# A hybrid decoder layer on one core: the norm of k as a part of its own ahead of the head pair's stage

## The chip, the core and the metric

The kernel runs on one core of a Trainium2 chip. The metric is the device time of one execution in microseconds (us); three runs of the kernel before took 1516.64, 1517.29 and 1518.45 us, the median is 1517.29 us. Five engines work side by side, each through its own queue in order: TensorE (PE for matmuls, PEld for its weight loads), VectorE (DVE), ScalarE (ACT), GpSimd (POOL) and SyncE (SP, which here only issues DMAs).

## What is computed

One layer of a decoder for a prompt of 512 tokens and 8 single-token samples, 520 columns in all, with 1024 channels. Two feed-forward blocks stand around a mixing block; the change lies in the mixing block alone, in the branch with a recurrent state. Cut to what matters here:

```python
h = rmsnorm(x, norm_mix);  z = h @ w_in              # 8448 columns: r | k | v | lora | conv B, C, u | gates
r, k, v, wd, ad, gd = token_shift(z_rwkv)
w = -softplus(-(decay_bias + tanh(wd) @ w_decay_up)) - 0.5;  decay = exp(-exp(w))
a = sigmoid(iclr_bias + ad @ w_iclr_up)
kk = heads(k * k_k)                                  # 16 heads of 64 channels
kk = kk / max(norm(kk, axis=-1), 1e-12)              # the norm that the change moves
k_mod = k * (1 + (a - 1) * k_a)
for t in range(T):                                   # per head, S is 64 x 64
    S = S * decay[t] - (S @ kk[t]) x (kk[t] * a[t]) + v[t] x k_mod[t]
    y[t] = S @ r[t]
```

The norm is a sum of 64 squares for each token and head, and the reciprocal root of it, by which `k * k_k` is then scaled.

## The kernel before

Activations lie with channels on the partitions, so a tile is 128 channels by 520 columns and holds two heads. A product with a block of 128 output columns of `w_in` is two halves of 260 columns, each 8 channel tiles by 3 matmuls (high by high, high by low, low by high part), 24 matmuls into one PSUM bank (lines 795 to 797). In the text one of these matmuls is called a step. Each half is read out of its bank by ACT and DVE before one of the three banks of the tag `mm` is used again.

`mix` (line 730) holds the mixing block, in which parts are Python generators, and a planner at its end (lines 1323 to 1386) writes them into one program. The parts are: `rkv(p)` makes k, then r, then v of head pair p (three products; `zshift` puts the shifted copy into the one buffer `mp` by ACT, line 808, and blends it by DVE, line 812); `conv` and `gate` are the other products; `stage(p)` prepares the recurrence of pair p in chunks of 32 tokens; `invert(p)` inverts the chunk's triangular matrices (32 x 32, many small DVE steps on the tile `F`, lines 1082 to 1093); `scan(q)` runs the 16 chunks for two pairs; `fin(p)` normalises its output; `sample` treats the 8 samples. Each `yield a, b` tells the planner how much TensorE time the lines above take by its reckoning, and how long to wait until this part goes on; a part starts when those named in `needs` are done. The products of one row ("big") fill the gaps, so that the planner lays the small matmuls of a stage between the steps of products. After that every engine takes its instructions in the order in which they stand in its queue.

`stage(p)` has four places that the text speaks of. **D**: the two small products for decay and rate (line 945, two halves, each with two banks of the tag `mw`), whose banks two tanh passes on ACT free (lines 946, 947). **K**: five small matmuls (line 968) that sum the squares, made by an ACT pass at the stage's start (line 943), per head and token; DVE then does the norm's Newton steps, 12 instructions of 104 x 10 elements (line 972 and the helper `rsqrt`, lines 49 to 54). **R**: ten small matmuls (line 995) that spread the norm back over 128 rows, into both banks of `mw`, and DVE multiplies k by it (line 998). **S**: 32 small matmuls for the chunk's inner products (line 1013), which need the chain of DVE passes after D: lines 951, 953, 988, 998, 1000, 1002, 1004 and 1005. So D, K, R and S stand in TensorE's queue in this order, with steps of products between them.

Of the kernel before, what the change touches and what calls it, by code (L numbers as in the profile page):

```python
# [8 lines left out]
F32 = mybir.dt.float32  # L9
F32R = mybir.dt.float32r  # L10
I32 = mybir.dt.int32
AF = mybir.ActivationFunctionType
ALU = mybir.AluOpType
AX = mybir.AxisListType

P = 128
D = 1024
NT = 8
# [27 lines left out]
def rsqrt(eng, pool, x, y):  # L46

    a = pool.tile([P, 16], F32, tag="nwt", name="nwt", bufs=2)[:x.shape[0], :x.shape[1]]
    eng.tensor_scalar(y.bitcast(I32), x.bitcast(I32), 1, None, ALU.logical_shift_right)
    eng.tensor_scalar(y.bitcast(I32), y.bitcast(I32), -1, 0x5F3759DF, ALU.mult, ALU.add)  # L50
    for _ in range(3):
        eng.scalar_tensor_tensor(a, y, -0.5, y, ALU.mult, ALU.mult)
        eng.tensor_tensor(a, a, x, ALU.mult)
        eng.scalar_tensor_tensor(y, a, 1.5, y, ALU.add, ALU.mult)


def hybrid_step(tc, I, O):
# [3 lines left out]
    with ExitStack() as top:  # L61
# [551 lines left out]
        with tc.tile_pool(name="mx", bufs=1) as mp:  # L613
# [12 lines left out]
            def wo_part():  # L626
# [13 lines left out]

            out = []
            mix(tc, nc, mp, pp, dp, low0, wprep, mwps, mmps, V, VV, I, O, HS, YM, ysplit, wo_part,
                ident, pmask)

# [85 lines left out]
def mix(tc, nc, mp, pp, dp, low0, wprep, mwps, mmps, V, VV, I, O, HS, YM, ysplit, wo_part, ident, pmask):  # L730

    hh, hl = [a for a, _ in HS], [b for _, b in HS]
    v1, act, pool = nc.vector, nc.scalar, nc.gpsimd
# [35 lines left out]
    def tt(name, bufs=1, w=N):  # L769
        return mp.tile([P, w], F32, tag=name, name=name, bufs=bufs)  # L770
# [4 lines left out]
    def c3(ap):  # L775
        return ap.rearrange("p (c t) -> p c t", t=C)
# [38 lines left out]
    zz, done = {}, {}  # L815
# [90 lines left out]
    GT = 104  # L906
    GROUPS = (slice(0, 4 * GT), slice(4 * GT, N))

    def parts(src, hi, lo):

        act.activation(hi, src, AF.Identity)
        pool.tensor_tensor(lo, src, hi.bitcast(F32), ALU.subtract)
        return hi, lo

    def t2(name, w=N, tags=(None, None)):
        return [mp.tile([P, w], F32R, tag=t or name + x, name=name + x) for x, t in zip("hl", tags)]

    def small(w, x, cs, name, rows=slice(0, P)):

        ps = mwps(name)  # L920
        terms = [(w[0], x[0]), (w[0], x[1])] + [(y, x[0]) for y in w[1:]]
        for i, (a, b) in enumerate(terms):
            nc.tensor.matmul(ps[:, :HN], lhsT=a[rows], rhs=b[rows, cs], start=i == 0, stop=i == len(terms) - 1)
        return ps[:, :HN]
# [5 lines left out]
    heads = blkr.bitcast(F32).rearrange("p (h x) -> p h x", h=2)[:, :, 0]  # L930
    ups = {}

    def wdi_load(p):
        raw = tt("wdi", 1, P)
        nc.sync.dma_start(raw, I["wdi"][:, p * P:(p + 1) * P])
        ups[p] = parts(raw, *t2("wd", P))

    def stage(p):

        r, k, vv = zz.pop(p)  # L940
        wdi = ups.pop(p)
        sg, a, kn = tt("sg"), tt("a"), tt("kn")
        act.activation(kn, k, AF.Square, scale=V("k_k", p))
        for cs in HALF:
            ps, ps2 = (small(wdi, lora, cs, x, rows) for x, rows in zip(("dec", "icl"), HP))
            act.activation(sg[:, cs], ps, AF.Tanh, bias=hka[:, 2, p:p + 1], scale=0.5)
# [15 lines left out]
        km = tt("km")  # L962
        act.activation(km, a, AF.Identity, scale=hka[:, 0, p:p + 1], bias=hka[:, 1, p:p + 1])
        pool.tensor_tensor(km, km, k, ALU.mult)

        ps = mwps("kn")
        for i in range(5):
            nc.tensor.matmul(ps[:GT, 2 * i:2 * i + 2], lhsT=kn[:, i * GT:i * GT + GT], rhs=heads, start=True, stop=True)
        rs = mp.tile([P, 10], F32, tag="rs", name="rs", bufs=2)
        yield 0.5, 0.5  # L970
        rx = mp.tile([P, 10], F32, tag="rx", name="rx", bufs=2)
        v1.tensor_scalar(rx[:GT], ps[:GT, 0:10], 1e-24, None, ALU.max)
        rsqrt(v1, mp, rx[:GT], rs[:GT])
        yield 0.0, 2.0
        if p > 3:
            yield ("fin", p - 4) if p % 2 else ("gate", p - 3)
        yield ("r", p)
# [8 lines left out]
        lam = mp.tile([P, NC], F32, tag="lam", name="lam", bufs=4)  # L986
        v1.tensor_copy(lam, eL[:, :, C])
        v1.tensor_tensor(AR[:, :, 1, :], c3(r[:, :T]), eL[:, :, 1:], ALU.mult)
        kk = kn
        kps = [mwps("kn") for _ in GROUPS]  # L990
        for cs, ps in zip(GROUPS, kps):
            for g in range(cs.start, cs.stop, GT):
                i = g // GT
                for h, hp in enumerate(HP):
                    nc.tensor.matmul(ps[hp, g - cs.start:g - cs.start + GT], rhs=ident[:GT, :GT], start=True, stop=True,
                                     lhsT=rs[:GT, 2 * i + h:2 * i + h + 1].broadcast_to([GT, 64]))
# [318 lines left out]
    def ys(m):  # L1315
# [7 lines left out]
    LAG = 1.2  # L1323
    WIN, DENSE, LIGHT = 8.0, 5500, 0.3
    make = {"scan": scan, "invert": invert, "stage": stage, "fin": fin, "sample": lambda p: sample(),
            "rkv": rkv, "conv": conv, "gate": gate, "low": lowrank, "ys": ys, "wo": lambda p: wo_part()}
    each = lambda kind: [(kind, p) for p in range(NT)]
    todo = {"scan": [("scan", q) for q in range(NT // 2)], "invert": each("invert"), "stage": each("stage"), "fin": each("fin"),
            "sample": [("sample", 0)], "ys": each("ys"), "big": []}
    bigs = {"gate": each("gate"), "rkv": each("rkv"), "conv": each("conv"), "wo": [("wo", 0)]}  # L1330
    live = {}

    def needs(kind, p):
        return {"stage": [("k", p)],
                "invert": [("stage", p)],
                "scan": [("invert", 2 * p), ("invert", 2 * p + 1)],
                "fin": [("scan", p // 2)] + [("gate", p - 2)] * (p > 1),
                "sample": [("stage", NT - 1)],
                "ys": [("gate", p), ("sample", 0)] + [(x, NT - 1) for x in ("rkv", "conv", "gate")],
                "wo": [("gate", NT - 1), ("conv", NT - 1)],  # L1340
                "rkv": [("stage", p - 2)] * (p > 1),
                "gate": [("fin", p)]}.get(kind, [])

    def ok(key):
        return all(x in done for x in needs(*key))
# [5 lines left out]
    while any(todo.values()) or any(bigs.values()) or live:  # L1351
# [5 lines left out]
        for row, q in todo.items():  # L1357
            if row not in live and q and ok(q[0]):
                key = q.pop(0)
                live[row] = [max([t] + [done[x] for x in needs(*key)]), make[key[0]](key[1]), key, None]  # L1360
# [120 lines left out]
```

## Time and profile before

The profiled execution took 1518.29 us, with a span of 1516.5 us from its first instruction to its last.

| engine | busy, us | share of the span |
|---|---|---|
| PE (matmul) | 1446.9 | 95% |
| PEld (weight load) | 1390.4 | 92% |
| DVE | 1076.5 | 71% |
| ACT | 770.1 | 51% |
| POOL | 398.5 | 26% |
| SP | issues DMAs only | |

The chain that ended last runs through PE for 75% of the span and through DVE for 15%. The mixing block takes up the stretch from about 405 to 1030 us. A row of the timeline is: start and duration in us, engine, line, operation, the tile written and the tiles read, and, in brackets, how long the engine had been idle before and what ended that. Matmuls overlap in the records, so their starts tell the pace, not their durations.

### The profile page before, as it was taken

The numbers are of one execution on the slowest core, as the hardware profiler recorded it, in microseconds if no ns is written. First come the engines' busy times: TensorE is split into PE (matmuls) and PEld (weight loads), VectorE is DVE, ScalarE is ACT, GpSimd is POOL, SyncE is SP. The second block draws the span as 40 slices with busy tenths as digits, with TensorE's granted clock in tenths as the row PEclk, the third lists the DMA queues.
The fourth block names the chain that finished last, engine by engine and source line by source line (L and its number), as shares of the span: only waits on it lengthen the run. The fifth ranks groups of instructions, "written<-read, shape, count | busy, mean of one in ns | idle before, by whom it ended". The sixth has DMA issues, their size and how long they took to land.

```text
span 1516.5 us, 36191 instructions
## 1 busy us (share of the span) xinstructions
PE 1446.9 (95%) x14772; PEld 1390.4 (92%) x14772; DVE 1076.5 (71%) x2349; ACT 770.1 (51%) x1352; POOL 398.5 (26%) x447
## 2 busy tenths in 40 slices
PE   8799999999999999999899999998989999999996
PEld 7799999999988988989888897898979999999996
DVE  7976665665698877859887659855697665666566
ACT  7655555555633443634444352244475555555643
POOL 1324334334231211201320113311023334333401
PEclk9899999999998999999999999999999999999998
DMA  5678888888332322313222222325246887888823
GB/s 180 153 167 182 181 183 183 182 191 181 123 106 68 82 66 53 97 45 83 67 67 66 73 78 87 100 88 168 91 125 161 178 185 176 192 180 172 169 68 103
DMA packets 116709, 193.44 MB, mean 128 GB/s; under 512 B 41992, under 2 KB 51208, under 8 KB 116288
## 3 DMA queue, kind: packets, MB, share of 16 engines
q1 hardware_dynamic: 92928, 140.80, 30.4%
q0 software_dynamic: 23616, 50.34, 20.7%
q8 instruction: 116, 1.90, 0.5%
q14 instruction: 49, 0.40, 0.1%
HBM read 179.83 MB, written 11.01 MB: 126 GB/s over the span
## 4 chain that ended last, share of the span: by engine, by line
PE 75%; DVE 15%; ACT 3%; issue 3%; DMA 2%; POOL 1%; SPq 0%; DVEq 0%; ACTq 0%; POOLq 0%
PE big L171 16%; PE big L173 16%; PE big L172 16%; PE big L795 6%; PE big L796 6%; PE big L797 5%; DVE lo L132 2%; PE xy L1171 1%; PE ds L1186 1%; PE xy L1177 1%; ACT hi L130 1%; PE ft L1123 1%; PE xy L1154 1%; DVE F L1090 1%; ACT W L1127 1%
## 5 line engine op out<-in xcount | busy, mean ns | idle before, releaser
L130 ACT ACTIVATE hi<-raw 128x512 fp32r<-128x512 f32 (+2 forms) x427 | 318.5, 749 | 323.6 <-PE big L172 171.2
L795 PE MATMUL big<-xh,hi 128*128 128x260 f32 x1040 | 310.5, 299 | 1.7 <-ACT cc L847 1.0
L797 PE MATMUL big<-xh,lo 128*128 128x260 f32 x1040 | 299.6, 289 | 2.0 <-DVE lo L132 2.0
L796 PE MATMUL big<-xl,hi 128*128 128x260 f32 x1040 | 300.8, 289 | 0.0
L132 DVE TENSOR_TENSOR lo<-raw,hi 128x512 fp32r<-128x512 f32 (+2 forms) x263 | 239.2, 912 | 62.1 <-ACT hi L130 57.0
L795 PEld LDWEIGHTS big<-xh,hi 128*128 128x128 f32 x1040 | 199.8, 192 | 11.6 <-ACT cc L847 1.2
L171 PE MATMUL big<-hh,hi 128*128 128x260 f32 x704 | 203.6, 289 | 3.0 <-DVE x L470 3.0
L797 PEld LDWEIGHTS big<-xh,lo 128*128 128x128 f32 x1040 | 199.3, 192 | 4.2 <-DVE lo L132 2.3
L796 PEld LDWEIGHTS big<-xl,hi 128*128 128x128 f32 x1040 | 200.1, 192 | 2.8
L172 PE MATMUL big<-hl,hi 128*128 128x260 f32 x704 | 199.5, 283 | 0.0
L173 PE MATMUL big<-hh,lo 128*128 128x260 f32 x704 | 199.5, 283 | 0.0
L171 PE MATMUL big<-th,hi 128*128 128x260 f32 x640 | 183.1, 286 | 8.5 <-ACT th L319 5.2
L172 PE MATMUL big<-tl,hi 128*128 128x260 f32 x640 | 182.8, 286 | 3.6 <-DVE tl L320 3.4
L173 PE MATMUL big<-th,lo 128*128 128x260 f32 x640 | 181.8, 284 | 0.0
L470 DVE SCALAR_TENSOR_TENSOR x<-big,x 128x260 f32<-128x260 f32 x176 | 74.5, 426 | 94.9 <-PE big L173 94.9
L171 PEld LDWEIGHTS big<-hh,hi 128*128 128x128 f32 x704 | 133.3, 189 | 6.5 <-DVE x L470 3.5
L173 PEld LDWEIGHTS big<-hh,lo 128*128 128x128 f32 x704 | 133.3, 189 | 0.0
L172 PEld LDWEIGHTS big<-hl,hi 128*128 128x128 f32 x704 | 133.2, 189 | 0.0
L171 PEld LDWEIGHTS big<-th,hi 128*128 128x128 f32 x640 | 121.5, 190 | 10.1 <-ACT th L319 6.0
L172 PEld LDWEIGHTS big<-tl,hi 128*128 128x128 f32 x640 | 121.6, 190 | 4.8 <-DVE tl L320 4.8
L171 PE MATMUL big<-xh,hi 128*128 128x260 f32 x400 | 114.9, 291 | 8.4 <-ACT hi L130 5.5
L166 DVE TENSOR_TENSOR raw<-raw 128x512 f32<-128x512 f32 x160 | 113.9, 713 | 12.6 <-DMA raw<-in_wu 5.6
(306 smaller groups left out, 3439.4 us busy)
## 6 DMA issues: line engine op xcount, KB each, us to landing
raw<-in_win SPq DMA_DIRECT2D x66, 512.0 KB, 3.8
raw<-in_wd SPq DMA_DIRECT2D x80, 256.0 KB, 2.9
lo<-in_wd POOLq DMA_DIRECT2D x72, 256.0 KB, 4.6
raw<-in_wu SPq DMA_DIRECT2D x24, 512.0 KB, 3.7
raw<-in_wg SPq DMA_DIRECT2D x23, 512.0 KB, 3.8
raw<-in_wg SPq DMA_DIRECT2D x40, 256.0 KB, 3.5
raw<-in_wu SPq DMA_DIRECT2D x40, 256.0 KB, 3.0
lo<-in_wg POOLq DMA_DIRECT2D x18, 512.0 KB, 5.7
```

The source lines that it names most:

```text
L130: nc.scalar.activation(self.hi[:, ks], self.raw[:, ks], AF.Identity)
L132: self.eng.tensor_tensor(self.lo[:, ks], self.raw[:, ks], self.hi[:, ks].bitcast(F32), ALU.subtract)
L166: nc.vector.tensor_tensor(self.raw, a.raw, b.raw, ALU.add)
L171: nc.tensor.matmul(ps[:, :HN], lhsT=hi, rhs=x[0], start=first, stop=False, skip_group_check=True)
L172: nc.tensor.matmul(ps[:, :HN], lhsT=hi, rhs=x[1], start=False, stop=False, skip_group_check=True)
L173: nc.tensor.matmul(ps[:, :HN], lhsT=lo, rhs=x[0], start=False, stop=last, skip_group_check=True)
L470: nc.vector.scalar_tensor_tensor(X[m][:, cs], ps, 0.5, X[m][:, cs], ALU.mult, ALU.add)
L795: nc.tensor.matmul(ps[:, :HN], lhsT=hi[:, k, :], rhs=hh[k][:, cs], start=k == 0, stop=False)
L796: nc.tensor.matmul(ps[:, :HN], lhsT=hi[:, k, :], rhs=hl[k][:, cs], start=False, stop=False)
L797: nc.tensor.matmul(ps[:, :HN], lhsT=lo[:, k, :], rhs=hh[k][:, cs], start=False, stop=k == nk - 1)
L1090: v1.tensor_tensor(f, f, ft[:, :, q0:, :j], ALU.add)
L1123: nc.tensor.matmul(ps[qd, i * 128:i * 128 + 96], lhsT=GM[qd, i, 96:], rhs=GM[qd, i, 0:96], start=False, stop=True, skip_group_check=True)
```

## The change

The square, K and the Newton steps leave `stage` and become a generator `norm(p)`, a row of its own in the planner. It needs only k of pair p, and `stage(p)` now needs `norm(p)`. The squares go into a tile of the tag `gt` (one buffer, also used by the lowrank, conv and gate products) in place of `kn`; the reciprocal roots wait in `rss`. Within the stage the yield that was 2.0 long in the planner's reckoning, with the one for K ahead of it, becomes one of 0.5, and `kn` is first written at line 998's multiplication.

```diff
+    rss = {}
+
+    def norm(p):
+
+        k = zz[p][1]
+        sq = tt("gt")
+        act.activation(sq, k, AF.Square, scale=V("k_k", p))
+        yield 0.0, 0.8
+        ps = mwps("kn")
+        for i in range(5):
+            nc.tensor.matmul(ps[:GT, 2 * i:2 * i + 2], lhsT=sq[:, i * GT:i * GT + GT], rhs=heads, start=True, stop=True)
+        rs = mp.tile([P, 10], F32, tag="rs", name="rs", bufs=2)
+        yield 0.5, 0.5
+        rx = mp.tile([P, 10], F32, tag="rx", name="rx", bufs=2)
+        v1.tensor_scalar(rx[:GT], ps[:GT, 0:10], 1e-24, None, ALU.max)
+        rsqrt(v1, mp, rx[:GT], rs[:GT])
+        rss[p] = rs
+        yield 0.0, 2.0
+
     def stage(p):
 
         r, k, vv = zz.pop(p)
         wdi = ups.pop(p)
-        sg, a, kn = tt("sg"), tt("a"), tt("kn")
-        act.activation(kn, k, AF.Square, scale=V("k_k", p))
+        sg, a = tt("sg"), tt("a")
...
         pool.tensor_tensor(km, km, k, ALU.mult)
-
-        ps = mwps("kn")
-        for i in range(5):
-            nc.tensor.matmul(ps[:GT, 2 * i:2 * i + 2], lhsT=kn[:, i * GT:i * GT + GT], rhs=heads, start=True, stop=True)
-        rs = mp.tile([P, 10], F32, tag="rs", name="rs", bufs=2)
-        yield 0.5, 0.5
-        rx = mp.tile([P, 10], F32, tag="rx", name="rx", bufs=2)
-        v1.tensor_scalar(rx[:GT], ps[:GT, 0:10], 1e-24, None, ALU.max)
-        rsqrt(v1, mp, rx[:GT], rs[:GT])
-        yield 0.0, 2.0
+        yield 0.0, 0.5
         if p > 3:
             yield ("fin", p - 4) if p % 2 else ("gate", p - 3)
         yield ("r", p)
...
-        kk = kn
+        kk, rs = tt("kn"), rss.pop(p)
...
     def needs(kind, p):
-        return {"stage": [("k", p)],
+        return {"norm": [("k", p)],
+                "stage": [("norm", p)],
                 "invert": [("stage", p)],
```

What this does to the queues is seen best at two places. In TensorE's queue of stage 5 before, D (`icl`) is followed by K (`kn<-blkr`, after the transposes `yt` of a `fin` part), and R (`kn<-cst,rs`) comes only after 31 steps more:

```order
L923 MATMUL icl<-lora_5319,wdh 128x260
L923 MATMUL icl<-lora_5318,wdl 128x260
L795 MATMUL big<-xh_4982,hi 128x260
L796 MATMUL big<-xl_4983,hi 128x260
L1228 MATMUL yt<-cst,AR 64x64 x16
L968 MATMUL kn<-blkr,kn 104x2 x5
L797 MATMUL big<-xh_4982,lo 128x260
```

In the same queue at the same stage after the change, where line 1004 is what was 995:

```order
L923 MATMUL icl<-lora_5319,wdh 128x260
L923 MATMUL icl<-lora_5318,wdl 128x260
L796 MATMUL big<-xl_4975,hi 128x260
L797 MATMUL big<-xh_4974,lo 128x260
L795 MATMUL big<-xh_4976,hi 128x260
L796 MATMUL big<-xl_4977,hi 128x260
L797 MATMUL big<-xh_4976,lo 128x260
L1004 MATMUL kn<-cst,rs 64x104 x10
```

R now follows D after five steps; K has left this place and stands 29 steps behind the last step of k's product, in the second half of r's. In VectorE's queue of stage 6 before, the last Newton steps (`nwt`, `rs`) stand among `invert` steps on `F`, a weight's low part (`lo`) and the reading out of a gate (`ym`), all ahead of line 988's multiplication:

```order
L54 SCALAR_TENSOR_TENSOR rs<-nwt,rs 104x10
L1088 TENSOR_TENSOR ft<-F_5326,Mr 128x2x3x5
L52 SCALAR_TENSOR_TENSOR nwt<-rs 104x10
L132 TENSOR_TENSOR lo<-raw,hi 128x1024
L53 TENSOR_TENSOR nwt<-nwt,rx 104x10
L895 SCALAR_TENSOR_TENSOR ym_5279<-gt,AR 128x252
L54 SCALAR_TENSOR_TENSOR rs<-nwt,rs 104x10
L900 SCALAR_TENSOR_TENSOR gS<-gt,gS 128x8
L988 TENSOR_TENSOR AR<-r,eL 128x16x32
```

In VectorE's queue of pair 6 after the change, the steps stand right behind the blending of k (first row), and line 952, once 972, is their first:

```order
L812 SCALAR_TENSOR_TENSOR k<-big,omm,mp 128x260
L952 TENSOR_SCALAR rx<-kn 104x10
L812 SCALAR_TENSOR_TENSOR r<-big,omm,mp 128x260
L49 TENSOR_SCALAR rs<-rx 104x10
L50 TENSOR_SCALAR rs<-rs 104x10
L52 SCALAR_TENSOR_TENSOR nwt<-rs 104x10
```

The first half of r now stands behind the step that waits for K.

## Rows read from the trace of the kernel before

**Rows 1.** Windows: busy us (count) of PE, PEld, DVE, ACT, POOL; clock; DMA.

```profile
405.00:1030.00 625.00, 598.30 (x7938) 552.92 (x7937) 482.49 (x1255) 264.36 (x538) 128.10 (x194) 0.98 0.28 79
```

**Rows 2.** The same view, five windows of 10 us.

```profile
450.00:460.00 10.00, 6.51 (x48) 5.61 (x46) 8.96 (x39) 4.17 (x10) 0.96 (x4) 0.88 0.35 113
460.00:470.00 10.00, 10.00 (x56) 10.00 (x56) 6.81 (x23) 4.79 (x11) 2.39 (x5) 0.60 0.28 51
...
770.00:780.00 10.00, 7.32 (x55) 6.88 (x54) 9.34 (x36) 3.32 (x7) 0.71 (x1) 0.76 0.18 52
780.00:790.00 10.00, 10.00 (x123) 9.79 (x123) 7.62 (x20) 2.13 (x5) 3.95 (x5) 0.90 0.28 66
1020.00:1030.00 10.00, 10.00 (x85) 10.00 (x85) 4.07 (x6) 3.75 (x7) 0.00 (x0) 1.00 0.23 68
```

**Rows 3.** Waits of PE, 405 to 1030: total us, times, longest us.

```profile
PE kn L995 <- DVE rs L54: 5.2, 2, 2.7
PE dec L923 <- ACT sg L946: 3.4, 2, 2.8
...
PE kn L995 <- DVE mp L811: 1.9, 1, 1.9
```

**Rows 4.** Groups by line: shapes, count | busy us, mean ns | idle before, releaser.

```profile
L1013 PE MATMUL sc<-AR,BK 64*64 64x64 f32 x512 | 17.1, 219 | 1.2 <-DVE BK L1005 1.2
...
L953 DVE TENSOR_TENSOR_SCAN sg<-smask,sg 128x512 f32<-128x512 f32 x8 | 11.0, 1380 | 0.0
L995 PE MATMUL kn<-cst,rs 104*64 104x104 f32 x160 | 9.8, 273 | 7.0 <-DVE rs L54 5.2 <-DVE mp L811 1.9
L968 PE MATMUL kn<-blkr,kn 128*104 128x2 f32 x80 | 9.1, 239 | 0.1
...
L946 ACT ACTIVATE sg<-dec,hka 128x260 f32<-128x260 f32 x16 | 7.6, 474 | 5.5 <-PE icl L923 3.8 <-PE dec L923 1.4
...
L943 ACT ACTIVATE kn<-k,vec 128x520 f32<-128x520 f32 x8 | 5.8, 726 | 6.9 <-PE bon L923 4.1 <-DVE k L812 2.9
L1002 DVE SCALAR_TENSOR_TENSOR a<-a,kn 128x520 f32<-128x520 f32 x8 | 5.5, 691 | 0.0
...
L52 DVE SCALAR_TENSOR_TENSOR nwt<-rs 104x10 f32<-104x10 f32 x24 | 4.0, 165 | 0.2
```

**Rows 5.** Timeline of stage 6, from its second D to its R.

```profile
766.03 0.28 PE L923 MATMUL icl<-lora,wdl 64*128 64x260 f32 x1
...
769.37 0.42 DVE L951 TENSOR_SCALAR sg<-sg 128x520 f32<-128x520 f32 x1
...
769.71 0.21 DVE L1088 TENSOR_TENSOR ft<-F,Mr 128x36 f32<-128x36 f32 x1
...
775.21 0.16 DVE L54 SCALAR_TENSOR_TENSOR rs<-nwt,rs 104x10 f32<-104x10 f32 x1
...
775.52 0.79 PE L995 MATMUL kn<-cst,rs 104*64 104x104 f32 x6 [2.69 <-DVE rs L54]
```

**Rows 6.** Timelines of pairs 1 and 6: last steps of k, its blending, its square.

```profile
444.15 0.28 PE L797 MATMUL big<-xh,lo 128*128 128x260 f32 x1
...
450.34 0.49 DVE L812 SCALAR_TENSOR_TENSOR k<-big,omm,mp 128x260 f32<-128x260 f32 x1
...
450.86 0.73 ACT L943 ACTIVATE kn<-k,vec 128x520 f32<-128x520 f32 x1 [2.87 <-DVE k L812]
...
450.88 0.39 PE L795 MATMUL big<-xh,hi 128*128 128x260 f32 x1 [0.69 <-DVE k L812]
...
457.77 0.48 ACT L808 ACTIVATE mp<-big,vec 128x260 f32<-128x260 f32 x1 [4.23 <-DVE F L1090]
...
458.67 0.58 PE L923 MATMUL dec<-lora,wdh 64*128 64x260 f32 x1 [2.79 <-ACT sg L946]
...
732.43 0.28 PE L797 MATMUL big<-xh,lo 128*128 128x260 f32 x1
...
736.80 0.48 DVE L812 SCALAR_TENSOR_TENSOR k<-big,omm,mp 128x260 f32<-128x260 f32 x1
```

More of the change, by code (lines that the diff above doesn't have):

```diff
@@ L1325, in mix @@
     make = {"scan": scan, "invert": invert, "stage": stage, "fin": fin, "sample": lambda p: sample(),
-            "rkv": rkv, "conv": conv, "gate": gate, "low": lowrank, "ys": ys, "wo": lambda p: wo_part()}
+            "rkv": rkv, "conv": conv, "gate": gate, "low": lowrank, "norm": norm, "ys": ys, "wo": lambda p: wo_part()}
     each = lambda kind: [(kind, p) for p in range(NT)]
-    todo = {"scan": [("scan", q) for q in range(NT // 2)], "invert": each("invert"), "stage": each("stage"), "fin": each("fin"),
+    todo = {"scan": [("scan", q) for q in range(NT // 2)], "invert": each("invert"), "norm": each("norm"), "stage": each("stage"), "fin": each("fin"),
             "sample": [("sample", 0)], "ys": each("ys"), "big": []}
```

## The prediction, made before the changed kernel was run

> **What bounds the kernel now.** I read the windows first, then TensorE's waits, then the groups by line and two pieces of the timeline. From 405 to 1030 us, the mixing block, PE is busy for 598.3 of 625 us and DVE for 482.5 [rows 1]: TensorE bounds this stretch, and an edit is worth only what it takes from PE's idle time or gives back to its clock. In a window without a wait PE starts 85 steps in 10 us [rows 2], 0.12 us a step.
>
> Of PE's waits in the block the largest one belongs to this change: R stands idle for the last Newton step, 5.2 us in two places and 1.9 in a third, where DVE had another small copy in hand [rows 3]. S, a little later in a stage, waits 1.2 us for the last pass of its DVE chain [rows 4]. Together that is 8.3 us. Stage 6 shows how it comes about: its second D ends at 766.31, DVE takes up the stage at 769.37 and the norm's last step ends at 775.37; R starts at 775.52 after 2.69 us of idle PE [rows 5]. The windows from 770 to 790 then show clocks of 0.76 and 0.90 [rows 2], a mixture of its two levels, 1.2 and 2.4 GHz; that cost 2.4 + 1.0 = 3.4 us more. So the most that can go is 11.7 us.
>
> The rest of PE's waits have another cause: DVE is late as such. In pair 1, k's last step starts at 444.15 but k is blended only at 450.83, 6.7 us later; PE then waits 0.69 us for the bank, and at D 2.79 us, since the tanh passes stand on ACT behind a shift copy that had waited 4.23 us for DVE [rows 6]. The clock of 0.88 and 0.60 there [rows 2] costs 1.2 + 4.0 = 5.2 us.
>
> **The change part by part.** No work is added. The square is the same ACT pass (0.73 us), K the same matmuls (9.1 / 8 = 1.1 us a stage), the Newton steps the same 12 short instructions (line 52's take 165 ns) [rows 4]. The norm issues no DMA, nothing of it runs on POOL, and nothing moves past SP's queue. Costed at nothing: the square's new tile `gt`, because in every stage the last reader of it in the program comes before k; if ACT had to wait for it, the price would be about one such pass, 0.73 us. What counts is where things now stand.
>
> *R.* In the order of the changed kernel, the norm is done long before R, which stands 12 steps behind D in stages 0, 1, 2 and 6, fewer in 3 and 5. R needs two banks of `mw`, and D's two tanh passes of 0.47 us each [rows 4] free them, so 12 steps (1.4 us) are enough and five (0.6 us) are about 0.5 us short. All of the old 7.1 us at R can go.
>
> *S.* But S moves closer to D as well, from 69 to 99 steps down to 44 to 92 (stage 4 aside, which waits for a gate), and DVE's chain between them is only relieved of the short Newton steps. For each stage I summed DVE's queue from line 951 to the chain's last pass: each instruction by the mean of its line, from the scan's 1380 ns over the passes of about 690 (five like line 1002's) down to 165, less 0.08, because a next one starts that much before the recorded end (769.71 against 769.79) [rows 4, 5]. To it comes the way from D through the second tanh, 1.2 us at best. Against it stand TensorE's steps at 0.12, R at 9.8 / 8 = 1.2 and whatever else lies between. Stage 6 after the change: 25 instructions, 8.8 us, plus 1.2 is 10.0, against 66 steps and R, 9.1: S waits 0.8. The others: 0.5 (stage 0), none (1), 1.5 (2), 0.8 (3), none (4), 0.6 (5), 0.7 (7). That is 4.9 us. The same sum on the old order gives 4.1 at R and S, where 8.3 were measured, so it is a low end. With the delay from D to line 951 that each stage showed before (3.06 us in stage 6 [rows 5], 0.5 to 4.0 in the others) the new order gives 8.7. I take the middle, 6.8: DVE's shortage in a stage mostly stays, and PE meets it at S instead of at R.
>
> *K.* This wait is new. Before, PE reached K without a wait (0.1 us in all [rows 4]), since k was done long ago. Now K stands 19 to 35 steps behind k's last step (81 in pair 3), and there k must first pass the shift copy on ACT, the blending on DVE and the square on ACT. From k's last step to the blended k took 2.3 to 7.5 us in the eight pairs, 6.7 in pair 1 and 4.9 in pair 6 [rows 6]; square and handovers add 0.9. Pair 1: 7.6 against 31 steps, 3.7 us: PE waits 3.9. Pair 6: 5.8 against 30 steps, 3.6: it waits 2.2. In the same way 0.7 in pairs 2 and 5 each; none in the others, where more steps, S or pieces of a scan lie between. That is 7.5 us. Behind K in PE's queue stand the products of r, and behind line 952 in DVE's queue the blending of r, whose bank PE needs two halves later; the square holds up the next shift copies on ACT, as it did before (2.87 us in pair 1 [rows 6]). The low end is nothing: part of this is the same lateness of DVE that PE already meets later, and in pair 1 the 0.69 and 2.79 us would be paid at K instead. Taking off these two I get 4.0, which I use.
>
> By the Trainium skill, "TensorE: Matmul & The Clock Gate", part 2, step by step, matmuls stay in program order and only weight loads are pulled ahead. The trace agrees: at 450.88 a product that waits for its bank holds up all behind it [rows 6]. If matmuls could pass K, K would cost nothing and the sum below would come out 4.0 lower; by the rule it is what it is.
>
> *Clock.* The two waits of 2.7 and 2.8 us were followed by stretches at the lower level [rows 2, 5, 6]. With waits at K of up to 3.9 us I give back half of the 3.4 us, 1.7; the ends are nothing and another stretch like that of pair 1, 5.2.
>
> *Sum*, against the profiled execution of 1518.29 us (its span of 1516.5 and 1.8 around it), which lies 1.0 above the median; differences carry over, so I add them to the median of 1517.3: -8.3 (R and S) - 3.4 (clock) + 6.8 (S) + 4.0 (K) + 1.7 (clock) = +0.8. **1518.1 us.** What lies behind is that the planner packs the stages into less product work: the last `fin` now comes 66 steps earlier, and these steps are left for the end of the block, where PE was busy for 10.00 us in a window with DVE at 4.07 [rows 2]. There they fill nothing, while DVE has the same work over a shorter run of steps.
>
> **The rivals.** *Faster:* R's waits go and DVE, freed of the chain through K, makes up for it: S waits only 4.9, K not at all, the clock stays up. -8.3 - 3.4 + 4.9 = -6.8, **1510.5**. For it: R's three waits are real, and in stage 6 the norm's last step ended 6.0 us after DVE had taken up line 951 (769.37 to 775.37 [rows 5]), which is long for 12 short instructions. Against it: k's lateness in pairs 1 and 6 [rows 6].
>
> *Slower:* K takes the place of R. PE stands in its queue for a k that has not yet come through ACT and DVE. Its whole price is 7.5 and S costs 6.8; the clock falls as often as before: -8.3 + 6.8 + 7.5 = +6.0, **1523.3**. It decides from about 4.5 us at K on. With S at 8.7 it is +7.9, 1525.2.
>
> *It does not do what it says:* K and the Newton steps could have stayed next to R if the scheduler had put them back. The order excludes it; 0.02, with no change in time.
>
> **How the numbers follow.** About 0.2%, 3.0 us, is what a measurement of this kernel can tell from no change. Unchanged (1514.3 to 1520.3) 0.36, and the 0.02 goes with it; faster 0.30; slower 0.32. The terms known to within 4 us each leave 1 in 10 below 1509.5 and 1 in 10 above 1527, the slower case with the high end of S (+7.9) and the 1.7 of the clock on top; the range reaches to these.
>
> **What would show it.** Right, if in the changed kernel line 1004 (R) has no more than 1.5 us of idle PE before it, line 1022 (S) 5 to 9 us, and line 948 (K) 2 to 8 us, most of it in pairs 1 and 6, released by ACT's square. The faster case is shown by S and K below 6 us together; the slower one by K above 4.5 us, and half clock behind it. What would make it wrong altogether: waits of the scans and of `sample`, which I leave as they are although the order changes there too, since nothing in the rows gives a direction.

## The result, and the profile of the changed kernel

The changed kernel takes 1536.4 us (median of six runs, 1530.8 to 1548.5) against 1517.2 for the kernel before; the ratio is 1.0132, with a 95% interval of 1.0103 to 1.0160. It is slower, by 19 us, and outside the range that I gave (1509.5 to 1527).

The profiled execution took 1542.6 us, 6 above the median; its span is 24.0 longer than that of before. First the PE lines of the two pages (busy us, share of the span, instructions), before and after; the spans are 1516.5 and 1540.5.

```profile
PE 1446.9 (95%) x14772; PEld 1390.4 (92%) x14772; DVE 1076.5 (71%) x2349; ACT 770.1 (51%) x1352; POOL 398.5 (26%) x447
```

```profile
PE 1457.0 (95%) x14772; PEld 1399.0 (91%) x14772; DVE 1081.8 (70%) x2349; ACT 762.4 (49%) x1346; POOL 393.6 (26%) x448
```

The same 14772 matmuls keep PE busy for 10.1 us more, and the rest of the span, in which PE stands, grew from 69.6 to 83.5, by 13.9. So there are two losses of like size: PE stands longer, and it takes longer over the same work. All of it lies in the mixing block. The windows that answer to [rows 1] and [rows 2], the second at the places where the changed kernel waits:

```profile
405.00:1030.00 625.00, 585.74 (x7746) 538.59 (x7745) 477.93 (x1240) 249.51 (x520) 124.25 (x192) 0.96 0.27 75
```

```profile
440.00:450.00 10.00, 7.37 (x64) 7.16 (x62) 9.59 (x22) 4.31 (x9) 1.84 (x5) 1.00 0.44 107
450.00:460.00 10.00, 10.00 (x74) 9.59 (x73) 8.33 (x46) 2.82 (x6) 0.72 (x3) 0.83 0.28 93
740.00:750.00 10.00, 7.19 (x42) 7.19 (x43) 8.73 (x19) 3.27 (x8) 2.65 (x4) 0.66 0.23 66
...
800.00:810.00 10.00, 8.13 (x44) 8.13 (x45) 6.80 (x25) 1.21 (x2) 0.29 (x2) 0.66 0.27 59
```

PE's mean clock in these 625 us went from 0.98 [rows 1] to 0.96. The block itself ends some 24 us later than before. Now PE's waits, 405 to 1052 us (total us, times, longest), which answer to [rows 3]; then the groups by line that answer to [rows 4]:

```profile
PE kn L948 <- ACT gt L944: 7.4, 4, 2.6
PE gu L923 <- DVE kn L1007: 5.3, 1, 5.3
PE ds L1195 <- DVE UV L1189: 5.2, 9, 1.2
PE big L797 <- DVE lo L132: 4.1, 6, 1.1
PE ft L1132 <- issue: 3.0, 4, 1.3
```

```profile
L1022 PE MATMUL sc<-AR,BK 64*64 64x64 f32 x512 | 16.6, 219 | 1.6 <-DVE ft L1097 1.6
...
L948 PE MATMUL kn<-blkr,gt 128*104 128x2 f32 x80 | 9.0, 238 | 7.4 <-ACT gt L944 7.4
L1004 PE MATMUL kn<-cst,rs 104*64 104x104 f32 x160 | 8.9, 258 | 0.0
...
L944 ACT ACTIVATE gt<-k,vec 128x520 f32<-128x520 f32 x8 | 5.8, 725 | 20.4 <-DVE k L812 20.4
```

R (line 1004) waits nowhere any more; 7.0 of idle time stood there before [rows 4]. D's 3.4 us behind ACT [rows 3] are gone too. K (line 948) waits 7.4; S (line 1022) waits 1.6, by the profile for a step of `invert` (`ft`) on DVE and not for its own chain; ACT stands 20.4 us at the Squares (line 944) for k, where 2.9 of 6.9 were for k before [rows 4]. The rest is at places the change doesn't name: `gu` of `fin` waited 1.1 and 0.2 before and waits 5.3, the scan's `ds` 1.5 and now 5.2, `big` behind `lo` 2.0 and now 4.1. These rows of before were not shown ahead:

```profile
PE big L797 <- DVE lo L132: 2.0, 2, 1.1
...
PE ds L1186 <- DVE UV L1180: 1.5, 3, 1.0
...
PE gu L923 <- ACT AR L1230: 1.1, 1, 1.1
```

How K comes to wait is seen in pair 1, at the place that answers to [rows 6] (start, duration, engine, line; in brackets the idle time ahead and what ended it):

```profile
446.61 1.23 DVE L132 TENSOR_TENSOR lo<-raw,hi 128x1024 fp32r<-128x1024 f32 x1
...
448.02 0.49 DVE L812 SCALAR_TENSOR_TENSOR k<-big,omm,mp 128x260 f32<-128x260 f32 x1
...
448.61 0.73 ACT L944 ACTIVATE gt<-k,vec 128x520 f32<-128x520 f32 x1 [3.27 <-DVE k L812]
...
449.39 1.08 PE L948 MATMUL kn<-blkr,gt 128*104 128x2 f32 x10 [2.63 <-ACT gt L944]
```

DVE has transposes and `lo` in its queue ahead of the blending of k; ACT stands 3.27 us at the Square for it, PE 2.63 at K for the Square. In stage 5, which answers to [rows 5] for R, R runs without a wait right behind D, and then holds both banks of `mw` until DVE, busy with `invert`, then with a `lo`, a gate and the stage's own first passes, comes to the kk multiply:

```profile
735.38 1.11 PE L1004 MATMUL kn<-cst,rs 104*64 104x104 f32 x20
...
742.13 0.85 DVE L1007 SCALAR_TENSOR_TENSOR kn<-k,vec,kn 128x416 f32<-128x416 f32 x2
...
742.81 0.58 PE L923 MATMUL gu<-sgd,guh 128*128 128x260 f32 x1 [5.29 <-DVE kn L1007]
```

### The profile page after: what moved, and what is told of

It reads as the page before. It is cut to its first block, busy times and chain, and to the rows that moved or that the text cites. A ratio compares the mean times of both kernels' runs of the same rounds, so it can differ in the third digit from the quotient of the medians.

```text
span 1540.5 us, 36162 instructions
## 1 busy us (share of the span) xinstructions
PE 1457.0 (95%) x14772; PEld 1399.0 (91%) x14772; DVE 1081.8 (70%) x2349; ACT 762.4 (49%) x1346; POOL 393.6 (26%) x448
## 5 line engine op out<-in xcount | busy, mean ns | idle before, releaser
L171 PEld LDWEIGHTS big<-th,hi 128*128 128x128 f32 x640 | 121.4, 190 | 10.1 <-ACT th L319 6.0
```

The costliest lines, as they stand in the source:

```text
L171: nc.tensor.matmul(ps[:, :HN], lhsT=hi, rhs=x[0], start=first, stop=False, skip_group_check=True)
```

## The experiments

All runs, with the median, the ratio to the kernel before (95% interval), and from the profiled execution PE's busy time and the rest of its span. The last column is counted from the timeline: stretches of PE of over 4 us in the mixing block that hold no step of a product (no matmul on `big`), how many and us together, each from the start of its first matmul to the end of its last. The count is mine, the other columns are those of the results and the profiles.

| run | median us | ratio | PE busy | PE idle | no product |
|---|---|---|---|---|---|
| before | 1517.2 | | 1446.9 | 69.6 | 1, 4 |
| changed | 1536.4 | 1.0132 (1.0103 to 1.0160) | 1457.0 | 83.5 | 4, 23 |
| 1 K later | 1518.6 | 0.9995 (0.9981 to 1.0009) | 1439.6 | 72.1 | 1, 5 |
| 2 old distance D to R | 1526.6 | 1.0047 (1.0032 to 1.0062) | 1448.7 | 76.0 | 3, 14 |
| 3 both | 1520.9 | 1.0014 (1.0003 to 1.0026) | 1448.8 | 72.3 | 3, 17 |
| 4 before, LAG 1.25 | 1528.7 | 1.0060 (1.0044 to 1.0076) | 1451.6 | 75.0 | 4, 18 |
| 5 norm moved alone | 1540.1 | 1.0137 (1.0108 to 1.0166) | 1459.3 | 79.1 | 3, 15 |
| 6 the same, K later | 1528.4 | 1.0073 (1.0056 to 1.0089) | 1452.6 | 75.7 | 1, 6 |
| 7 changed, K later in its order | 1533.8 | 1.0104 (1.0066 to 1.0143) | 1446.2 | 77.7 | 3, 17 |
| 8 changed, gu first | 1543.2 | 1.0173 (1.0136 to 1.0211) | 1459.9 | 81.1 | 5, 27 |
| 9 norm moved alone, K by D | 1522.4 | 1.0041 (1.0025 to 1.0057) | 1451.3 | 69.9 | 0 |
| 10 changed, K by D in its order | 1553.2 | 1.0222 (1.0186 to 1.0259) | 1479.0 | 79.0 | 8, 47 |
| 11 before, second Square | 1518.8 | 1.0011 (0.9999 to 1.0023) | 1447.9 | 71.4 | 1, 4 |
| 12 K later still | 1520.9 | 1.0035 (1.0014 to 1.0056) | 1447.8 | 73.4 | 1, 5 |
| 13 before, second Square and K | 1531.4 | 1.0082 (1.0062 to 1.0102) | 1451.5 | 74.2 | 3, 14 |
| 14 before, no Newton | 1515.9 | 0.9978 (0.9965 to 0.9990) | 1445.6 | 67.9 | 0 |
| 15 changed, no Newton | 1552.5 | 1.0203 (1.0165 to 1.0241) | 1464.6 | 88.0 | 9, 47 |
| 16 K later, two edits | 1514.1 | 0.9959 (0.9945 to 0.9973) | 1442.0 | 70.4 | 2, 9 |
| 17 changed, products as before | 1536.4 | 1.0138 (1.0112 to 1.0165) | 1452.1 | 79.5 | 3, 15 |
| 18 before, products as changed | 1533.6 | 1.0106 (1.0077 to 1.0135) | 1451.5 | 74.0 | 3, 12 |

The median of before moves between 1515.7 and 1518.6 with the chip; the ratio is against the runs beside each. For runs 1, 7, 13, 17 and 18 the profiled execution was the fastest of its kernel (1513.5, 1525.7, 1527.6, 1533.6, 1527.3), for runs 6, 10 and 15 the slowest (1530.1, 1559.8, 1554.7), so that their PE columns lie to that side.

**Runs 1 to 4: the planner draws the order.** Three one-number edits of the changed kernel, and one of the kernel before.

```diff
-        yield 0.0, 0.8      # norm: between Square and K
+        yield 0.0, 3.0      # runs 1 and 3
-        yield 0.0, 0.5      # stage: between km and R
+        yield 0.0, 2.9      # runs 2 and 3
-    LAG = 1.2
+    LAG = 1.25              # run 4, the kernel before
```

> The changed kernel, except that the norm's part waits longer between the Square on ACT and K (yield 0.0, 3.0 for 0.0, 0.8), so that K stands some 2.6 us of plan later in PE's queue. Theory A (K's early place costs): K's 7.4 us of waits go, and the half-clock stretches behind two of them (450.46, 3.41 us; 802.03, 6.83 us; half of them lost, 5.1 us) go too: 12 us below the changed kernel, about 1524. Theory B (the stage is pressed together, R directly behind D, so that R holds both mw banks and DVE's work is packed): R is 12 steps behind D as in the changed kernel, so K's waits go but the time stays within 4 us of the changed kernel's 1536, or falls by the 7.4 us alone at most. Theory C (every new order draws its own time, whatever is moved): anything from 1515 to 1545, with the waits at other places than in the changed kernel.

> The changed kernel with K early as it is, but the stage waits as long of plan between its km and R as in the kernel before (yield 0.0, 2.9 for 0.0, 0.5; with the planner's factor 1.2 that is 3.5 us, as 0.5 + 0.5*1.2 + 2.0*1.2 was). R is then 27 to 39 steps behind D instead of 12. Theory A: K's waits (7.4 us) and the clock lost behind them stay: within 4 us of 1536. Theory B: the 5.3 us wait of gu behind R's banks, its half-clock stretch (3.4 us lost) and part of the 9 us of other waits of scans and invert go: 1518 to 1528. Theory C: anything from 1515 to 1545.

> Both edits together: K later (0.0, 3.0) and the old distance ahead of R (0.0, 2.9). Theory A: as K later alone, about 1524. Theory B: as the old distance alone or 7 us less. A and B both true: their gains add, 1510 to 1518, at or below the kernel before, since R's 7.1 us of waits and S's 1.2 are gone as well. Theory C: no sum to be seen, anything from 1515 to 1545.

> The kernel before, norm in the stage as it was, with one number of the planner changed: LAG 1.25 for 1.2 (every wait of the parts that are not the products' is 4% longer in the plan). What is computed and which instruction follows which inside a part stays. Theories A and B: the norm is where it was, so the time is within 4 us of 1517. Theory C: the order is another, so the time is another, by as much as the changed kernel's 19 us either way; over 8 us off 1517 speaks for C.

K later gives all of the loss back, more than A's 12 us; K's waits fell to 2.4. The old distance (run 2) gives 10 us back with K's waits at 9.1, as B has it, and the two don't add. Run 3 still waits 7.2 us at K, as long as the changed kernel, and is only 2 us slower than the runs of before beside it, so a wait of that length at K need not come with a loss of that size. And run 4 is 10 us slower with the norm untouched. That is C's mark, and it says why runs 1 to 3 settle little: each number made the planner draw the whole order anew. In the changed kernel's order the scans' matmuls stand 45 steps from their old places on average, and its products come as `rkv3 rkv4 rkv5 conv1`, where before, as in runs 1 to 3 and 12, `conv1` stood behind `rkv3`.

**Runs 5 to 10: one thing moved in a fixed order.** So I replaced the planner's loop by the list of its choices. With the changed kernel's own list this gives the changed kernel's instructions in the same order; from then on single steps could be moved.

```diff
-    while any(todo.values()) or any(bigs.values()) or live:
-        ...
+    plan = """ rkv0*18 norm0 stage0 ... """
+    for word in plan.split():
+        key, n = (word.split("*") + ["1"])[:2]
+        if key not in live:
+            live[key] = make[key[:-1]](int(key[-1]))
+        for _ in range(int(n)):
+            next(live[key], None)
```

Runs 5, 6 and 9 take the list of before, with the norm's steps put in. Around pair 1 (Square, K and Newton are the first three `norm1`):

```diff
 run 5:  rkv1*3 norm1 rkv1 stage0 rkv1*2 norm1 rkv1 stage0 rkv1*3 norm1 stage0 ...
 run 6:  rkv1*3 norm1 rkv1 stage0 rkv1*3 stage0 rkv1*3 stage0 rkv1*3 stage0 rkv1 norm1 rkv1*2 stage0 rkv1*2 norm1 ...
 run 9:  rkv1*3 norm1 stage0 rkv1*3 ... stage0 invert0 norm1 stage1 rkv1*2 stage1 norm1 ...
```

> The order of the kernel before kept, and the norm alone moved: the planner's loop is replaced by the list of parts in the order in which the kernel before ran them, with the norm's three steps (Square, K, Newton) put where rkv's product for k is there, as in the changed kernel, and taken out of the stage. R stands 3 to 17 steps earlier, the other small products move by about one step on average, at most 22. Theory A (K's early place costs by itself, wherever the rest stands): K waits about 7 us as in the changed kernel and loses clock behind two waits, R's 7.1 and S's 1.2 are gone: about 1517 - 8.3 + 7.4 + 5.1 = 1521. Theory B (the stage pressed together costs): it isn't pressed here, 1509 to 1514. Theory C (the loss is in the order that the planner drew, in which scans, inverts and fin stand 24 to 65 steps elsewhere): those waits are absent, so the time is the sum of the prediction without its order terms, -8.3 - 3.4 + 4.0 + 1.7 = -6.0, 1511; within 1508 to 1517.

> As the norm moved alone in the order of the kernel before, with K 3.6 us of plan behind the Square instead of 0.96. Theory A: K's waits and their clock go, R's and S's stay away: 1517 - 8.3 = 1509, some 12 us below the run with K at its early place. Theories B and C: K's waits are worth their own length at most, so 0 to 7 us below it, 1506 to 1512.

> The order of the kernel before kept, and the norm alone moved, as in the run before with that order, but less far: Square 4 us of plan ahead of the stage's first D products, K right ahead of them, Newton 1.1 us of plan behind K (pairs 0 and 4, whose k comes together with the stage: K 3.6 us of plan behind the Square). R stands as in that run. Theory A1 (PE stands at K because its Square isn't done): K finds its Square done, R's 7.1 and S's 1.2 us are gone: 1517 - 8.3 = 1509, within 1505 to 1513, 30 us under the norm moved to the early place. Rival C (taking the norm off the way between D and R costs by itself, wherever K stands, since DVE's queue gets R's and S's work sooner): R, S or the inverts wait instead, 1517 to 1530.

In the order of before, the move alone costs 21 to 23 us (by the ratio and by the medians): A's direction and more than its size, against B and C. Waits of run 5, and the chain at K of pair 3:

```profile
PE kn L948 <- ACT gt L944: 13.6, 4, 4.6
PE kn L1004 <- DVE AR L1244: 3.4, 1, 3.4
...
PE kn L1004 <- DVE lam L996: 2.2, 1, 2.2
```

```profile
537.81 1.23 DVE L132 TENSOR_TENSOR lo<-raw,hi 128x1024 fp32r<-128x1024 f32 x1
...
539.23 0.49 DVE L812 SCALAR_TENSOR_TENSOR k<-big,omm,mp 128x260 f32<-128x260 f32 x1
...
539.75 0.73 ACT L944 ACTIVATE gt<-k,vec 128x520 f32<-128x520 f32 x1 [6.24 <-DVE k L812]
...
540.53 1.89 PE L948 MATMUL kn<-blkr,gt 128*104 128x2 f32 x10 [4.48 <-ACT gt L944]
```

K later (run 6) takes half of it back, though K still waits 7.1 us there; K by D (run 9) takes back 15 us by the ratios and 18 by the medians, with K's idle time at 0.6. But run 9 is still 5 to 6 us slower than before, not 8 faster: the rival's side. R's waits are as long as in run 5, 5.6 us, again for other releasers than the Newton steps, and D's second half stands 2.3 us for the bank that K holds until line 952:

```profile
L1004 PE MATMUL kn<-cst,rs 104*64 104x104 f32 x160 | 9.7, 261 | 5.6 <-DVE AR L1244 2.5 <-DVE mp L811 1.9 <-DVE F L1099 1.2
...
L948 PE MATMUL kn<-blkr,gt 128*104 128x2 f32 x80 | 8.2, 228 | 0.6 <-ACT gt L944 0.5
```

```profile
PE icl L923 <- DVE rx L952: 2.3, 1, 2.3
```

Runs 7, 8 and 10 take the list of the changed kernel: K some steps later; `gu` of `fin3` ahead of stage 5's R; Square and K by D.

```diff
-rkv1*3 norm1 rkv1 stage0 rkv1*2 norm1 stage0 rkv1*2 norm1 rkv1 ...
+rkv1*3 norm1 rkv1 stage0 rkv1*2 stage0 rkv1*3 stage0 rkv1*3 stage0 rkv1 norm1 ...    (run 7, and so for each pair)
-gate2*2 stage5*3 invert4 gate2 fin3
+gate2*2 stage5*2 fin3 stage5 invert4 gate2*2                                         (run 8)
-rkv1*3 norm1 rkv1 stage0 rkv1*2 norm1 ... stage0 invert0 stage1 rkv1*2 stage1
+rkv1*3 norm1 stage0 ... stage0 invert0 norm1 stage1 rkv1*2 stage1 norm1              (run 10, and so for each pair)
```

> The order of the changed kernel kept (its own list of parts), and only K and the Newton steps behind it put 3.6 us of plan behind the Square instead of 0.96 (K moves by up to 19 steps, most of the rest by none). Theory A: K's 7.4 us and the 5.1 us of clock behind two of its waits go: 1536 - 12.5 = 1524, and the 18 us of the earlier run, in which the planner drew a new order, were mostly this. Theory B or C: at most the 7.4 us, 1529 to 1537, and the earlier run's gain came from its other order.

> The order of the changed kernel kept, with one edit: fin's gu products (and the multiplies behind them) stand ahead of stage 5's R instead of some ten steps behind it, so that they don't wait for the mw banks that R holds until DVE has reached the kk multiply. Theory B (that wait is a large part): the 5.3 us go and the half-clock stretch of 6.83 us at 740.59 too (3.4 us lost): 1536 - 8.7 = 1528. Theory C (PE would only wait for DVE at the next place, since DVE is behind there): 1533 to 1537, with a wait of 3 us or more for DVE between 735 and 755.

> The order of the changed kernel kept, with Square, K and Newton put as in the run before this one: Square 4 us of plan ahead of the stage's D, K right ahead of D. Theory A1: K's 7.4 us and the 5.1 us of clock behind two of its waits go: 1536 - 12.5 = 1524 (1519 to 1528). Rival C (the changed kernel's order is slow for other reasons: scans, inverts, gu): 1530 to 1540, with K's waits gone.

Run 7 tells little: its K waits are still 6.8 us, so K was not far enough off. Run 8 refutes B: the 5.3 us did not go; R took 4.7 of them, for the same DVE queue, and the time of 1543.2 lies even above what C had (1533 to 1537):

```profile
PE kn L1004 <- DVE AR L1244: 4.7, 1, 4.7
```

Run 10 goes against A in this order, and its 1553.2 lies above the rival's range (1530 to 1540) too. K waits nowhere, and it is 14 to 17 us slower than the changed kernel (by the ratios and by the medians), although PE stands 4.5 us less: PE is busy for 22.0 us more. The test isn't clean, since D, right behind K, now stands for K's bank where K stood before:

```profile
PE icl L923 <- DVE rx L952: 4.7, 2, 2.8
```

Three windows of run 10, and the same of before:

```profile
530.00:540.00 10.00, 8.50 (x174) 7.91 (x177) 2.77 (x5) 3.08 (x6) 0.34 (x3) 0.84 0.49 123
540.00:550.00 10.00, 10.00 (x120) 8.28 (x108) 1.80 (x7) 4.46 (x10) 0.00 (x0) 0.50 0.11 15
550.00:560.00 10.00, 10.00 (x95) 8.71 (x94) 6.04 (x21) 3.87 (x11) 2.47 (x3) 0.50 0.10 26
```

```profile
530.00:540.00 10.00, 8.79 (x208) 8.19 (x207) 7.58 (x13) 3.07 (x6) 0.29 (x2) 1.00 0.42 111
540.00:550.00 10.00, 9.69 (x132) 8.72 (x133) 4.75 (x14) 6.60 (x14) 0.23 (x2) 1.00 0.26 81
550.00:560.00 10.00, 9.74 (x131) 8.26 (x129) 9.45 (x30) 5.57 (x16) 1.23 (x4) 1.00 0.23 55
```

In run 10 PE runs K, D, R, a scan's and an `invert`'s matmuls there with 19 product matmuls among them (three lines of 7, 6 and 6 in 540 to 560), and at 1.2 GHz throughout; in the kernel before 93 stand in 20 us of the same kind (536 to 556), at 2.4.

**Runs 11 and 13 to 15: one cost by itself.** Runs 11 and 13 leave the kernel before as it is, in its own order, and add a part whose results nobody reads. Runs 14 and 15 take the three Newton steps out of `rsqrt`.

```diff
+    def norm(p):
+        sq = tt("gt")
+        act.activation(sq, zz[p][1], AF.Square, scale=V("k_k", p))
+        yield 0.0, 0.8
+        ps = mwps("kn")                      # these three lines in run 13 alone
+        for i in range(5):
+            nc.tensor.matmul(ps[:GT, 2 * i:2 * i + 2], lhsT=sq[...], rhs=heads, ...)
-    for _ in range(3):                       # rsqrt, runs 14 and 15
+    for _ in range(0):
```

> The kernel before in its own order with its norm where it was, and a second Square for each pair at the early place (as soon as rkv's product for k is there) into the buffer gt, which nobody reads: eight ACT instructions of 0.7 us, nothing else. Theory A1 (K on PE is what costs): the time stays, 1515 to 1520; ACT standing 3 to 6 us on the Square is no loss. Theory A2 (the Square holds up ACT's queue, which evicts the products' sums and lets the banks go): 1525 or more, a good part of the 23 us that the norm moved alone has lost.

> The kernel before in its own order with its norm where it was, and for each pair a second Square and a second K (five matmuls into an mw bank, read by nobody) at the early place; the run with the second Square alone took 1518.8. Theory A1 (PE stands at the early K, behind DVE's k and ACT's Square): the 13.6 us of K waits and the 11 us of clock of the run with the norm moved alone come here too, while R's waits stay: 1535 to 1545. Rival D (what that run lost came from R and the multiplies behind it standing earlier): 1517 to 1523.

> The kernel before with the three Newton steps left out (nine DVE instructions for each pair, 12.3 us of DVE in all; the norm is then the first guess only, so the result differs). Theory W (what waits at R is worth its length): 5.2 us of R waits behind the Newton steps go, 1510 to 1513. Theory V (DVE is late at all these places, and a wait that goes comes back a little later, as in the run with K ahead of D, where R's waits went from 7.1 to 5.6 and the whole stayed): 1514 to 1519, R's waits turned to other DVE instructions.

> The changed kernel with the three Newton steps left out as well (the result differs). PE waits nowhere for them in the changed kernel. Theory W: no gain but by DVE's being 12 us freer: 1532 to 1538. Theory V (DVE's lateness is what PE waits for everywhere): a gain as large as in the kernel before or larger, 1520 to 1531.

The early Square alone costs nothing that shows, though ACT stands 17 us for it: A2 falls. The Square's group in run 11, then PE's first two waits in run 13:

```profile
L941 ACT ACTIVATE gt<-k,vec 128x520 f32<-128x520 f32 x8 | 5.8, 728 | 17.1 <-DVE k L812 17.1
```

```profile
PE kn L945 <- ACT gt L941: 7.9, 4, 4.0
PE kn L1005 <- DVE rs L54: 7.5, 4, 2.7
```

With K behind it the kernel loses 11 to 13 us more. But here K is added, not moved: at 1.1 us a pair [rows 4] up to 8.6 of these are the matmuls themselves, and the standing is worth 2 us or more. So run 13 has A1's direction and not its size; it came out between A1's range and D's. The early place is priced better by runs 5 and 9, which have R within 7 steps of the same place and differ by 15 to 18 us. But there Square, K and Newton move together. The Square by itself is free (run 11); K on PE and the Newton steps on DVE, ahead of the blending of r, no run takes apart.

Without Newton the kernel before gains 2.6 us, although R's waits for `rs` were 5.2 [rows 3]; R now waits for the next thing:

```profile
L995 PE MATMUL kn<-cst,rs 104*64 104x104 f32 x160 | 9.7, 262 | 3.3 <-DVE AR L1235 2.5 <-DVE lam L987 0.8
```

That is V. Run 15 is neither V nor W: with less work on DVE the changed kernel is 11 to 16 us slower, at 1552.5. Like run 10 it lies at half clock where PE was never idle:

```profile
546.00:556.00 10.00, 10.00 (x92) 8.78 (x93) 2.05 (x9) 4.50 (x10) 0.00 (x0) 0.50 0.09 15
```

**Runs 17 and 18: the sequence of the products.** Both let the planner draw, but give it the products' parts in a fixed sequence.

```diff
-    bigs = {"gate": each("gate"), "rkv": each("rkv"), "conv": each("conv"), "wo": [("wo", 0)]}
+    bigs = {"rkv": [("rkv", 0)], "all": [...]}
     run 17, the changed kernel:  rkv3 conv1 rkv4 gate0 rkv5 gate1 conv2 rkv6 gate2 gate3 rkv7 ...
     run 18, the kernel before:   rkv3 rkv4 rkv5 conv1 gate0 gate1 conv2 gate2 gate3 rkv6 rkv7 ...
```

> The changed kernel, its planner drawing the order, but with the parts of the big products taken in the sequence of the kernel before (... rkv3 conv1 rkv4 gate0 rkv5 ... rkv6 gate2 gate3 rkv7 ...), where the planner of the changed kernel took rkv3 rkv4 rkv5 conv1 and put rkv6 behind gate3. K, D, R stand as in the changed kernel up to pair 3, R directly behind D. Theory O (the planner's other sequence of the products is what slows the changed kernel): the waits and half-clock stretches between 530 and 610 go, and what is left is the early K: 1520 to 1528. Theory A1 (the early K alone): no change, 1532 to 1540.

> The kernel before, its norm in the stage and its planner as they were, but with the parts of the big products taken in the sequence of the changed kernel (rkv3 rkv4 rkv5 conv1 gate0 gate1 conv2 gate2 gate3 rkv6 rkv7). Theory O: slower than before by 8 us or more with no norm moved, 1525 to 1540. Theory A1: 1515 to 1520.

Run 18 comes out as O has it: 16 to 18 us slower with no norm moved. But the planner draws the small matmuls anew around the products: the scans' stand 30 steps from their old places on average, 26 in run 4, so the sequence is not varied by itself. Run 17 speaks against O: the old sequence brings the changed kernel nothing. `gu` waits as in the changed kernel, K 5.2 us for its 7.4:

```profile
PE gu L923 <- DVE kn L1007: 5.6, 1, 5.6
PE kn L948 <- ACT gt L944: 5.2, 3, 2.6
```

**Runs 12 and 16: a version that beats both.** Run 12 puts `yield 0.0, 6.0` where run 1 has 3.0. Run 16 is the list of run 1 with pair 1's K and S moved on, since they waited 1.9 and 3.5 us there.

```diff
-rkv1*2 norm1 stage0 rkv1*2 norm1 rkv1 stage0 rkv1*4 stage0
+rkv1*2 stage0 rkv1*3 stage0 rkv1*4 norm1*2 stage0
-invert0 stage1 invert0 conv0*2 invert0 conv0*2 ...
+invert0 conv0*2 invert0 conv0*2 ... stage1        (S of pair 1, 30 product steps on)
```

> The changed kernel, its planner drawing the order, with yield 0.0, 6.0 for 0.0, 0.8 between Square and K (0.0, 3.0 gave 1518.6 and left 2.4 us of K waits). Theory A1: the last 2.4 us go as well, 1514 to 1518. Rival C (the order that the planner draws decides, K's lag only shakes it): anywhere from 1510 to 1535.

> The order of the kernel with K later (yield 0.0, 3.0; 1518.6) kept, with two edits at its longest waits: pair 1's K 15 steps later (it waited 1.9 us) and pair 1's S 30 steps later (it waited 3.5 us). Theory W: these 5.4 us go, 1513, which beats both kernels. Theory V: the waits come back at the next places, 1516 to 1520.

Run 12 waits nowhere at K and is no faster than run 1 (1520.9, where A1 had 1514 to 1518): S waits 5.8 us there. Run 16 has W's time: 1514.1, 0.4% under the kernel before (0.9945 to 0.9973), with PE busy for 4.9 us less than before and idle for 0.8 more. It is the fastest of all, and what it gains over before is busy time. Its waits are not W's: the two that were edited went, but others came, 2.2 us of `big` for `lo` where S had stood and 2.0 at another pair's K, so that PE stands only 1.7 us less than in run 1:

```profile
PE big L797 <- DVE lo L132: 5.6, 5, 2.2
...
PE kn L948 <- ACT gt L944: 2.7, 3, 2.0
```

## Why the prediction was wrong

The step that failed is the one that put everything outside R, S, K and the clock at nothing: 16.6 us of waits came there. With it the clock came out with the wrong sign. Term by term:

**R and S: -8.3, half right.** R's waits went to nothing, as said. What failed is their worth. In run 9 the waits for the Newton steps go in the old order, with 0.6 us to pay at K, but R stands 5.6 us for other work of DVE and the kernel is slower; in run 14 their cause is taken out altogether and 2.6 us come back. DVE is late at these places as such, and PE stands at the next thing that DVE owes. I had written that sentence for k and not used it for R.

**S: +6.8, mis-sized.** S waits once, 1.6 us (line 1022). My sums of DVE's queue against PE's steps gave 4.9 to 8.7. That PE loses so much elsewhere that S is seldom early is only argued.

**K: +4.0, right in size, partly by luck.** K waits 7.4 where 7.5 was the full price, and D's 3.4 us went, which I had taken off for lateness that PE pays at K instead. But the pairs differ: 2.6 us in pair 1 (3.9 said), 1.7 in pair 2 (0.7 said), 2.6 in pair 7 at 801.87 (none said), and none in pair 6 (2.2 said). And a wait's length is not its worth: in run 5 the place cost 15 to 18 us for 13.6 of waiting, in run 3 all that was lost was 2 us, with 7.2 of waiting.

**These terms together** are -7.1 (R) + 0.4 (S) - 3.4 (D) + 7.4 (K) = -2.7 us, against the +2.5 of my sum. By these lengths alone PE would have stood less than before.

**The rest: left as it was, and there it failed.** Of PE's 13.9 us more of idle time, 13.9 + 2.7 = 16.6 lie at waits that I did not price: 4.0 at `gu`, 3.7 at `ds`, 2.1 at `big` behind `lo`, and small ones of scans, `invert`, `yt`. I named the scans' among them as what would make it wrong, and gave them nothing "since nothing in the rows gives a direction"; `gu` and `lo` I did not name. A missing direction is no zero. With the norm where it was, run 18 fixes another sequence of the products and run 4 changes one number of the planner: 16 and 10 us.

**Clock: -3.4 + 1.7, the wrong sign.** PE's busy time rose by 10.1. Most of that is clock: the granted 0.977 and 0.972 of the two profiled executions leave 34.9 and 43.1 us missing, 8 apart. (Not all busy time is: run 9, at 0.980, keeps PE busy for 4.4 us more than before.) I had tied the clock to the waits at R and K. Waits of 2.6 and 5.3 us do have half clock behind them (windows at 450, 740 and 800). But run 10 shows more loss with less waiting: 22 us of busy time more than the changed kernel at 4.5 us less idle time. What goes with it is the last column of the table: the changed kernel has 4 stretches of over 4 us without a product, before 1, run 10 has 8 and run 15 has 9. Over the twenty kernels the us in that column and the median time correlate with 0.89, without runs 10 and 15 with 0.77. That is no proof of a cause, since such a stretch also grows longer at half clock, and no run varied it alone.

**What the runs settle and what they don't.** Shown: moved alone in the old order, the norm costs 21 to 23 us, of which 15 to 18 are the early place of its parts (run 5 against 9), and 5 to 6 remain with K next to D, where D stands for K's bank. Shown as well: with no norm moved, another order drawn by the planner costs 10 us (run 4) or 16 to 18 (run 18, with the new sequence of the products). Either the early place or the new order could be the changed kernel's 19. They don't add: undoing one leaves the loss (run 17; run 10, at a worse clock and with D's new wait), and in the draw of run 1, with 2.4 us left at K and the old sequence, it is gone. So the cause of the 19 us stays open. Why the early place is worth 15 to 18 us in one order, while run 3 with 7.2 us at K lost 2 in all, has no explanation here; that PE would in either case stand for the same late DVE is only argued. The slower rival had one of the two mechanisms, K in PE's queue for a k not yet through DVE and ACT, and priced it at 7.5, by its waits alone, which came to +6.0 in its sum.

## What to carry to other kernels

An operation traced as soon as its input is "there" waits in its engine's queue for all that its input has still to pass: on an engine with time to spare (ACT stood 17 us at the second Square, at 1.0011 of the time) that is all but free, on the engine that sets the end it can cost more than the wait (run 5), so try it where its input has been done for some microseconds. Where a planner sets the order, first measure what another draw of the order costs (one number changed: 10 us) and give a forecast at least that width; to test one move, write the order out as a list and move that alone. Idle time ahead of an instruction is worth its length only if the engine that is waited for isn't also late for the next one.

## What was not expected of the hardware

TensorE stayed at 1.2 GHz while its column showed no idle time: in run 10 from 540 to 560, PE 10.00 of 10.00 in both windows at a clock of 0.50, after a window with 8.50. In the kernel before, a window with 8.79 at the same place was followed by two at 1.00. In the changed kernel one with 8.46 was followed by these two, with more idle time than run 10 and 48 steps of products in them:

```profile
540.00:550.00 10.00, 9.51 (x164) 7.90 (x158) 4.12 (x22) 6.10 (x14) 0.00 (x0) 1.00 0.17 34
550.00:560.00 10.00, 7.96 (x121) 7.13 (x118) 9.01 (x27) 4.97 (x13) 3.05 (x4) 1.00 0.03 7
```

The Trainium skill, "TensorE: Matmul & The Clock Gate", part 1, gives the lower level to an idle engine and the upper one to a busy one. The two windows of run 10 differ from it, if busy is what the profile's column counts; the measurement decides. What PE ran in them was, but for 19 steps of products, matmuls of 32x32 and 64x64 and the stage's small ones. Whether that is why stays open: no run varied it by itself.

The scatter of one program goes with the clock too. The six runs of the changed kernel lie between 1530.8 us at a mean clock of 0.983 and 1548.5 at 0.969. The 0.017 and 0.031 that these clocks lack of full speed are 26 and 48 us of the times, 22 apart, where the times differ by 17.7.
